# Half the blocks of attention weights transposed by VectorE and DMAs, in a two-layer RG-LRU and forgetting-attention trunk

## The chip, the cores and the metric

The kernel runs on one core of a Trainium2 chip. The metric is device time in microseconds (us) of one execution. A change is judged by the medians of runs of both kernels on the same chip. Engines are named as in the profile: PE (TensorE, matmuls), PEld (its weight loads), DVE (VectorE), ACT (ScalarE), POOL (GpSimd), SP (SyncE, which issues all the DMAs here).

## What is computed

The input x is 1024 positions by 1024 channels, in float32. Two residual layers and a last RMS norm are applied to it. Layer 0 is an RG-LRU branch of width 1536: a projection into a stream and a gate, a causal convolution of 4 taps, two block-diagonal gates, a linear recurrence along the sequence, a SiLU gate, and a projection back. Layer 1 is attention with 16 heads of 64, whose logits carry a bias of accumulated forget gates. Cut to what matters here:

```python
def fox_mixer(h, w_in, b_f, w_out):
    u = h @ w_in                       # q, k, v, gate (1024 each), 16 forget logits
    cum = cumsum(log_sigmoid(f_logit + b_f))
    # for each head and each block of 128 queries:
    logits = q_blk @ k.T / 8 + (cum_q - cum_k)
    p = softmax(where(kpos <= qpos, logits, -1e30))
    o = p @ v
    return (o * silu(gate)) @ w_out

def rms_norm(x, g):
    return x * rsqrt(mean(x * x) + 1e-6) * g
```

## The kernel before, in words

The whole kernel is transposed: channels lie on the 128 partitions, positions along the free dimension in two halves of 512. To keep the precision of float32, most operands are cut into a high part (a cast to the matmul's `fp32r`) and a low part (the rest, `to_hi` and `to_lo`, lines 84 to 98), and a product takes three matmuls: high by high, high by low and low by high. Raw weights land by DMA in tiles with the tag `wf` (4 buffers, lines 103, 268, 358, 532, 982) and are split into `wh` and `wl`.

**The norm.** `inv_rms` (line 142) sums squares with one-column matmuls (`col`), takes a root on ACT and a reciprocal on DVE, which gives one factor per position in a column `rms`. To have it as a row over all partitions, DVE multiplies the identity with each of the four columns (line 153) and one matmul with a matrix of ones turns that into `row` (lines 154 and 155). It is called four times.

**Layer 0** fills the first 455 us of the trace. Its loop over 12 blocks of channels loads raw weights, splits them and keeps PE supplied with projections.

**Layer 1.** `values` makes v for four heads at a time, `kq_units` makes q and k for a pair of heads, `g_units` the gate of a pair. For a head `hd` and a half `c` of the queries:

- `maxima(hd, c)` (line 708) takes four blocks of 128 queries, i = 4c to 4c+3, called rows here. For each, PE writes the scores S of the block against all (i+1) x 128 keys up to it, DVE masks them and finds the largest (line 731), and ACT writes the weights `p` = exp(...) into SBUF with their sums (line 736). Queries lie on the partitions.
- `weigh(hd, c)` (line 767) needs keys on the partitions. For two blocks of keys at a time, PE transposes each 128x128 block of `p` into PSUM (line 793, tile `pt`), ACT casts a high part `ph` (line 798), DVE subtracts a low part `pl` (line 801), and PE multiplies both with v into O (lines 781 and 782). The products of one step are issued only behind the transposes of the next step. Over a head there are 36 blocks to transpose.
- `scale` and `gated` multiply by the gate and the reciprocal sums on POOL. The result `yo` of a pair of heads is written to memory for the first six pairs (`y1d`, line 826). At heads 12 and later it is loaded again (`load_y`, line 861), split into parts (`split_loaded`, line 866), and multiplied with the output weights (`partial`, line 890).

The order on PE is written out by hand. In `run` and `ordered` (lines 838 to 850) a string is read letter by letter: "0" takes a step of `weigh`, "1" a row of `maxima`, "." two blocks (six matmuls) of projection work as fill. For heads 0 to 11 the two strings of a head are

```python
ORDER = "1.0.1.1.1.0.0", "10.1.0.1.01.0.0"
run(first, weigh(hd, 0), maxima(hd, 1), fill=fill)
run(second, weigh(hd, 1), maxima(hd + 1, 0), fill=fill, side=side)
```

and `LAST`, with more fill between, serves heads 12 to 15. The steps of PE are tied to this order by `tc.issue_after(pe[0].ins)`. The order on the other engines, SP's queue among them, is found by the framework's scheduler at build time. S and `pt` share two PSUM buffers (tag `S`, two banks each), O has two. Each row's `p` has one buffer of its own (`p0` to `p7`), `ph` and `pl` have three.

Of the kernel before, what the change touches and what calls it, by code (L numbers as in the profile page):

```python
# [17 lines left out]
P = 128  # L18
SEQ = 1024
# [19 lines left out]
def trunk(ctx: ExitStack, tc: tile.TileContext, xt, w0, wg, wo0, pc, gn, gf, w1, wv, wf, bf, wo1, out):  # L39
# [60 lines left out]
    def split_weights(src, shape, hi_eng, lo_eng, parts=wpool):  # L100
        n = shape[0] * shape[1]
        room = -(-n // 64) * 64
        a = wpool.tile([P, room], F32, tag="wf", name="wf", bufs=4)[:, :n]
        b = parts.tile([P, room], F32R, tag="wh", name="wh")[:, :n]
        c = parts.tile([P, room], F32R, tag="wl", name="wl")[:, :n]
        wt, hi, lo = (t.rearrange("p (a b) -> p a b", a=shape[0]) for t in (a, b, c))
        for part, sl in src:
            nc.sync.dma_start(wt[:, :, sl], part)
# [70 lines left out]
    with ExitStack() as l0:  # L179
# [87 lines left out]
        def split_gates(n):  # L267
            wt = wpool.tile([P, 4, P], F32, tag="wf", name="wgf", bufs=4)[:, :2]
# [87 lines left out]
        def out_weights(g, d0, parts=wpool):  # L356

            wt = wpool.tile([P, 4, P], F32, tag="wf", name="wf", bufs=4)
            for j in range(2):
# [137 lines left out]

    y1d = dram.tile([2, KT, P, HALF], F32, name="y1d")
    cumd = dram.tile([HEADS, 2, SEQ], F32, name="cumd")
    recd = dram.tile([HEADS, 8, P], F32, name="recd")  # L500

    with ExitStack() as l1:
# [24 lines left out]
        def value_weights(g, parts):  # L527

            waiting = []
            for k in range(0, KT + 2, 2):  # L530
                if k < KT:
                    wt = wpool.tile([P, 2, 256], F32, tag="wf", name="wf", bufs=4)
                    nc.sync.dma_start(wt, wv[g, :, k : k + 2])
                    waiting.append(wt)
# [105 lines left out]

        fz = const.tile([P, 8, HEADS], F32, name="fz")
        Vs = {}
# [7 lines left out]
        def forget(half):  # L650
# [7 lines left out]
            e_ = at.tile([HEADS, HALF], F32, tag="ph", name="e", bufs=3)  # L658
            parts = [at.tile([HEADS, HALF], F32R, tag=f"p{i + 2 * half}", name="cp", bufs=1) for i in (3, 4)]
            hi, lo = parts  # L660
# [45 lines left out]
        stats, ps_ = {}, {}  # L706

        def maxima(hd, c):

# [4 lines left out]
            sums = stats[hd]  # L714
            for i in range(4 * c, 4 * c + 4):
                n = (i + 1) * P
# [5 lines left out]
                for lo_, hi_ in ((0, min(n, HALF - o_)), (HALF - o_, n)):  # L722
# [11 lines left out]

                p = ps_[i] = at.tile([P, n], F32, tag=f"p{i}", name="p", bufs=1)
                seen[0] = nc.scalar.activation(  # L736
                    p, S[:, :n], AF.Exp, bias=m, scale=-1.0, accum_out=sums[:, i : i + 1]
                )
                yield
            if hd == HEADS - 1 or c == 1:  # L740
# [26 lines left out]
        def weigh(hd, c, sub=slice(0, HALF)):  # L767
# [9 lines left out]
            def products(j0, qlo, parts):  # L777
                for j, q, (ph, pl) in zip((j0, j0 + 1), qlo, parts):
# [3 lines left out]
                    matmul(o, v, pl, start=False, stop=j == nj - 1)  # L782

            held = None
            for j0 in range(0, nj, 2):
                A = ps.tile([P, 2, HALF], F32, tag="S", name="pt")
                qlo = [max(begin, j * P) for j in (j0, j0 + 1)]
                ns = [end - q for q in qlo]
                for jj in range(2):
                    ks = slice((j0 + jj) * P, (j0 + jj + 1) * P)  # L790
                    for q in range(qlo[jj], end, P):
                        o = q - qlo[jj]
                        transpose(A[:, jj, o : o + P], ps_[q // P][:, ks], ident)
                parts = []
                for jj in range(2):
                    a = A[:, jj, : ns[jj]]
                    ph, pl = (at.tile([P, HALF], F32R, tag=t, name=t, bufs=3)[:, : ns[jj]] for t in ("ph", "pl"))
                    to_hi(ph, a, nc.scalar)
                    parts.append((ph, pl))
                for jj, (ph, pl) in enumerate(parts):  # L800
                    to_lo(pl, A[:, jj, : ns[jj]], ph, nc.vector)
                if held:
# [11 lines left out]
        def gated(hd, c, sub=slice(0, HALF)):  # L814
# [10 lines left out]
            elif hd < 13:  # L825
                nc.sync.dma_start(y1d[c, pair], yo)

# [38 lines left out]
        def split_loaded(c):  # L866
            for pair in range(6):
                yh, yl = y1[c][pair]
                with tc.issue_after(seen[0].ins):
                    to_hi(yh, f32(yl), nc.scalar)  # L870
                with tc.issue_after(masked[0].ins):
                    to_lo(yl, f32(yl), yh, nc.vector)
                yield

        def beside(steps, first, more):

            for i, _ in enumerate(steps):
                if i >= first:
                    next(more, None)
                yield  # L880

# [39 lines left out]
        def turned(c, q):  # L921
# [9 lines left out]
            else:  # L931
                res = [tu.tile([P, SEQ], F32, tag="U1", name="res"), at.tile([P, SEQ], F32, tag="p7", name="res", bufs=1)]
            for b in range(2):
# [43 lines left out]
        def late():  # L977

            for half in range(2):
                wh, wl = (kqpool.tile([P, 8, P], F32R, tag=f"qk{p}{half}", name=f"wo{p}") for p in "hl")  # L980
                for b in range(2):
                    wt = wpool.tile([P, 4, P], F32, tag="wf", name="wf", bufs=4)
                    for d in range(2):
# [24 lines left out]
        for hd in range(HEADS):  # L1008
            pair = hd // 2
            if hd % 2 == 0:  # L1010
                if hd < 12:
                    fill = kq_units(pair + 1, ((1, (0, 1)), (0, (0,))))
                elif hd == 12:
                    pairs = ((0, 1), (2, 3), (4, 5), (6, 7))
                    todo = [(db, c) for two in pairs for c in range(2) for db in two]
                    splits = [split_loaded(c) for c in range(2)]
                    fill = chain(
# [122 lines left out]
```

## Time and profile before

| what | us |
|---|---|
| median of 3 runs | 1113.87 (1113.86 to 1114.06) |
| profiled execution, its own time | 1113.94 |
| its span, first to last instruction | 1112.2 |
| PE busy | 1101.9 |
| DVE busy | 755.0 |
| ACT busy | 582.4 |
| POOL busy | 166.1 |

In the rows of the profile, L57 is the line of the helper that issues every matmul and L61 that of the transposes, so work is told apart by tile: `gps` and `ups` are projections, `vps` v, S scores, `pt` the weights' transposes, O the products with v, `ops` output projections. "x7" after a name is a count of instructions, "a <- b" after a wait names what ended it. A busy time is a union of spans, so instructions that overlap count once.

### The profile page before, as it was taken

The page shows a single profiled execution, that of the slowest core. Times are in us where ns is not written, and L with a number is a line of the kernel's source. Part 1 is how long each engine was busy: PE and PEld are TensorE (multiplying, and loading weights), DVE is VectorE, ACT ScalarE, POOL GpSimd, SP SyncE. Part 2 cuts the span into 40 slices and gives each one's busy share as a digit, 9 for nine tenths or more (in the row PEclk, how much of TensorE's full clock was granted, in tenths as well). Part 3 has the DMA queues.
Part 4 walks back from the last instruction along what each step waited for, and adds up shares of the span by engine and source line. Part 5 has one row for each costly group of instructions (what it writes and reads, how often), then busy time and mean ns, then how long its engine had stood idle before and what let it go on. Part 6 is the DMA issues. An engine that isn't in the chain of part 4 may idle for free.

```text
span 1112.2 us, 15778 instructions
## 1 busy us (share of the span) xinstructions
PE 1101.9 (99%) x5697; PEld 935.1 (84%) x5697; DVE 755.0 (68%) x1266; ACT 582.4 (52%) x1075; POOL 166.1 (15%) x120
## 2 busy tenths in 40 slices
PE   9999999999999999999999999999999999999997
PEld 7787888888888888988888988889888898878886
DVE  8888755876669687756676566765667655576645
ACT  8487445355453665544555355544555544454435
POOL 1222212111111201421110100101002020010110
PEclk9999999999999999999999999999999999999999
DMA  6111111111112113443334224242142431655444
GB/s 239 48 57 43 51 54 43 48 53 42 62 35 75 48 54 129 129 112 118 101 90 103 91 69 109 72 113 96 53 122 75 103 108 38 185 159 185 142 147 189
DMA packets 63558, 105.43 MB, mean 95 GB/s; under 512 B 9364, under 2 KB 24340, under 8 KB 63480
## 3 DMA queue, kind: packets, MB, share of 16 engines
q1 hardware_dynamic: 63480, 104.42, 31.1%
q8 instruction: 45, 0.74, 0.3%
q14 instruction: 33, 0.27, 0.1%
HBM read 63.30 MB, written 15.93 MB: 71 GB/s over the span
## 4 chain that ended last, share of the span: by engine, by line
PE 93%; issue 3%; DVE 1%; ACT 1%; POOL 1%; DMA 1%; SPq 0%; DVEq 0%; POOLq 0%; ACTq 0%
PE gps L57 33%; PE ops L57 17%; PE ups L57 10%; PE vps L57 8%; PE S L57 6%; PE O L57 6%; PE pt L61 6%; PE turn L57 3%; PE gate L57 2%; POOL wl L98 1%; PE sscol L57 0%; DMA x<-in_xt 0%; DVE hl L232 0%; PE rsrow L57 0%; DMA wf<-in_w 0%
## 5 line engine op out<-in xcount | busy, mean ns | idle before, releaser
L57 PE MATMUL gps<-hh,wh 128*128 128x512 f32 x576 | 228.2, 396 | 0.0
L57 PE MATMUL gps<-hh,wl 128*128 128x512 f32 x576 | 225.6, 392 | 0.2 <-POOL wl L98 0.2
L57 PE MATMUL gps<-hl,wh 128*128 128x512 f32 x576 | 225.5, 392 | 0.0
L87 ACT CAST wh<-wf 128x512 fp32r<-128x512 f32 (+2 forms) x156 | 94.0, 607 | 141.8 <-PE gps L57 56.0
L736 ACT ACTIVATE p<-S,m 128x128 f32<-128x128 f32 (+7 forms) x128 | 94.9, 741 | 140.0 <-DVE m L731 139.1
L98 POOL TENSOR_TENSOR wl<-wf,wh 128x512 fp32r<-128x512 f32 (+1 forms) x60 | 95.6, 1600 | 382.2 <-ACT wh L87 321.7
L98 DVE TENSOR_TENSOR pl<-pt,ph 128x512 fp32r<-128x512 f32 (+1 forms) x198 | 98.7, 540 | 77.0 <-ACT ph L87 76.3
L57 PEld LDWEIGHTS gps<-hl,wh 128*128 128x128 f32 x576 | 108.2, 188 | 23.8
L57 PEld LDWEIGHTS gps<-hh,wl 128*128 128x128 f32 x576 | 108.5, 188 | 19.2 <-POOL wl L98 0.6
L57 PEld LDWEIGHTS gps<-hh,wh 128*128 128x128 f32 x576 | 108.5, 188 | 19.0
L731 DVE CUSTOM_DVE_ANT_0 S<-S,mask 128x128 f32<-128x128 f32 (+7 forms) x128 | 97.3, 760 | 34.2 <-PE S L57 29.6
L765 POOL TENSOR_TENSOR sg<-sg,recb 64x512 f32<-64x512 f32 x32 | 42.8, 1356 | 441.9 <-DMA recb<-recd 407.3
L87 ACT CAST ph<-pt 128x512 fp32r<-128x512 f32 (+1 forms) x198 | 83.5, 472 | 29.1 <-PE pt L61 23.9
L57 PE MATMUL S<-T,U 96*128 96x512 f32 (+7 forms) x384 | 91.7, 347 | 0.0
L98 DVE TENSOR_TENSOR wl<-wf,wh 128x512 fp32r<-128x512 f32 x96 | 68.3, 719 | 24.6 <-ACT wh L87 23.8
L375 DVE TENSOR_TENSOR x<-x,ops 128x512 f32<-128x512 f32 x80 | 54.1, 681 | 40.3 <-PE ops L57 40.3
L57 PEld LDWEIGHTS S<-T,U 128*128 128x128 f32 (+1 forms) x384 | 68.7, 189 | 12.5 <-ACT p L736 0.2
L61 PE MATMUL pt<-ident,p 128*128 128x128 f32 x576 | 79.2, 273 | 0.0
L61 PEld LDWEIGHTS pt<-ident,p 128*128 128x128 f32 x576 | 67.5, 140 | 11.5 <-issue 2.1
L57 PE MATMUL ups<-hh,wh 128*128 128x512 f32 x192 | 75.4, 394 | 1.0 <-ACT hh L89 0.4
L57 PE MATMUL ups<-hh,wl 128*128 128x512 f32 x192 | 75.0, 391 | 0.6 <-POOL wl L98 0.6
L57 PE MATMUL ups<-hl,wh 128*128 128x512 f32 x192 | 75.2, 391 | 0.2 <-DVE hl L232 0.2
(163 smaller groups left out, 2245.4 us busy)
## 6 DMA issues: line engine op xcount, KB each, us to landing
wf<-in_w SPq DMA_DIRECT2D x100, 256.0 KB
wf<-in_wo SPq DMA_DIRECT2D x64, 128.0 KB
U<-qkh SPq DMA_DIRECT2D x64, 128.0 KB
T<-qkh SPq DMA_DIRECT2D x28, 256.0 KB
x1d<-x SPq DMA_DIRECT2D x16, 256.0 KB
wf<-in_wv SPq DMA_DIRECT2D x16, 256.0 KB
U<-qkl SPq DMA_DIRECT2D x32, 128.0 KB
xp<-x1d SPq DMA_DIRECT2D x16, 256.0 KB
```

Of the source, the lines that this page charges most:

```text
L57: pe[0] = nc.tensor.matmul(*args, **kw)
L61: pe[0] = nc.tensor.transpose(*args)
L87: nc.scalar.copy(hi, src)
L98: return eng.tensor_tensor(lo, src, f32(hi), ALU.subtract)
L375: nc.vector.tensor_tensor(x, x, pt, ALU.add)
L731: masked[0] = nc.vector.tensor_tensor_reduce(S[:, :n], S[:, :n], mask[:, SEQ - n :], -1.0, -NEG, ALU.add, ALU.min, accum_out=m)
L736: seen[0] = nc.scalar.activation(p, S[:, :n], AF.Exp, bias=m, scale=-1.0, accum_out=sums[:, i : i + 1])
L765: nc.gpsimd.tensor_tensor(sg, sg, recs[hd // 2][rows, part], ALU.mult)
```

## The change

Rows 2, 3, 6 and 7 of a head, that is two of each four, no longer go through PE for most of their blocks. After exp, `turn_row` has DVE transpose the row's weights in blocks of 32x32 within each quarter of the partitions, into a tile `turn` (one buffer), and SP writes it to memory (`turnd`). When the second row of a pair is written, four DMAs, one for each group of 32 partitions of the result, read both rows back in such an order that the blocks stand transposed, over the place where the rows were (`two_rows`). This covers 3 blocks of keys of rows 2 and 3 and 7 of rows 6 and 7. The last block of rows 3 and 7 and all of rows 0, 1, 4 and 5 stay with PE. Rows 2 and 3 of head 0 stay with PE as well (`by_dma`). `maxima` takes its four rows from the last to the first.

In `weigh` each step now has a near part, from PE's transposes in PSUM, and a far part, from SBUF. Each is split by its own cast and subtraction, near parts first.

`inv_rms` drops the multiplications with the identity and the matmul with ones; four transposes of the column, read as a 128x128 tile by broadcast, write the row.

The results of the first six pairs of heads are split into high and low as soon as they are made, and both parts are written to memory and loaded later; `split_loaded` and `beside` go.

To make room, `wf` has 3 buffers in place of 4, and some small tiles share other tags.

```diff
-        a = wpool.tile([P, room], F32, tag="wf", name="wf", bufs=4)[:, :n]
+        a = wpool.tile([P, room], F32, tag="wf", name="wf", bufs=3)[:, :n]
...
-        nc.vector.reciprocal(rms, rms)
+        done = nc.vector.reciprocal(rms, rms)
+        row = ps.tile([P, HALF], F32, tag="O", name="rsrow")[:, : nb * P]
         for b in range(nb):
-            done = nc.vector.tensor_scalar(rs[:, b * P : (b + 1) * P], ident, rms[:, b : b + 1], None, ALU.mult)
-        row = ps.tile([P, HALF], F32, tag="O", name="rsrow")[:, : nb * P]
-        inst = matmul(row, onesf, rs, start=True, stop=True)
+            inst = transpose(row[:, b * P : (b + 1) * P], rms[:, b : b + 1].to_broadcast([P, P]), ident)
...
+        two_rows = {}
+        turnd = [dram.tile([P, 2, (4 * c + 3) * P], F32, name=f"turnd{c}") for c in range(2)]
+        def row_tile(i, n):
+            c, r = i // 4, i % 4 - 2
+            if r < 0:
+                return at.tile([P, n], F32, tag=f"p{i}", name="p", bufs=1)
+            size = (4 * c + 3) * P
+            if r:
+                two_rows[c] = at.tile([P, 2 * size + P], F32, tag=f"pp{c}", name="pp", bufs=1)
+            return two_rows[c][:, r * size : r * size + n]
+        def by_dma(hd, c):
+            return hd > 0 or c == 1
+        def turn_row(i, p):
+            c, r = i // 4, i % 4 - 2
+            nk = 4 * c + 3
+            t = at.tile([P, 7 * P], F32, tag="turn", name="turn", bufs=1)[:, : nk * P]
+            nc.vector.transpose(
+                t.rearrange("p (m k q) -> p k m q", m=4, q=32),
+                p[:, : nk * P].rearrange("p (k m q) -> p k m q", m=4, q=32),
+            )
+            nc.sync.dma_start(turnd[c][:, r], t)
+            if r == 0:
+                to = two_rows[c][:, : 2 * nk * P].rearrange("p (r b f) -> p r b f", r=2, b=4)
+                src = turnd[c].rearrange("(b p) r (m f) -> m p r b f", b=4, m=4)
+                for m in range(4):
+                    nc.sync.dma_start(to[32 * m : 32 * m + 32], src[m])
+        def far_rows(c):
+            return two_rows[c][:, : (8 * c + 6) * P].rearrange("p (b k q) -> p b k q", b=8, q=32)
...
-            for i in range(4 * c, 4 * c + 4):
+            for i in reversed(range(4 * c, 4 * c + 4)):
...
-                p = ps_[i] = at.tile([P, n], F32, tag=f"p{i}", name="p", bufs=1)
+                p = ps_[i] = row_tile(i, n)
...
+                if i % 4 > 1 and by_dma(hd, c):
+                    turn_row(i, p)
...
-                for jj in range(2):
-                    ks = slice((j0 + jj) * P, (j0 + jj + 1) * P)
-                    for q in range(qlo[jj], end, P):
-                        o = q - qlo[jj]
-                        transpose(A[:, jj, o : o + P], ps_[q // P][:, ks], ident)
...
+                near, far = [], []
+                for jj, j in enumerate((j0, j0 + 1)):
+                    rows = range(qlo[jj] // P, end // P)
+                    away = [i for i in rows if i % 4 > 1 and j < 4 * c + 3] if by_dma(hd, c) else []
+                    own = [i for i in rows if i not in away]
+                    for o, i in enumerate(own):
+                        transpose(A[:, jj, o * P : (o + 1) * P], ps_[i][:, j * P : (j + 1) * P], ident)
...
+                for lo in range(2):
+                    for (ph, pl), (src, to) in zip(parts, near):
+                        if to.stop:
+                            split(src, ph[:, to], pl[:, to], lo)
+                for lo in range(2):
+                    for (ph, pl), f in zip(parts, far):
+                        if f:
+                            j, b, to = f
+                            split(far_rows(c)[:, b, j], *(z[:, to].rearrange("p (b q) -> p b q", q=32) for z in (ph, pl)), lo)
...
-                nc.sync.dma_start(y1d[c, pair], yo)
+                yh = at.tile([P, HALF], F32R, tag="xp", name="yh", bufs=2)
+                with tc.issue_after(seen[0].ins):
+                    to_hi(yh, yo, nc.scalar)
+                with tc.issue_after(masked[0].ins):
+                    to_lo(yo.bitcast(F32R), yo, yh, nc.vector)
+                for part, y in enumerate((f32(yh), yo)):
+                    nc.sync.dma_start(y1d[c, pair, part], y)
...
-                nc.sync.dma_start(f32(pair_of_y(c, pair)[1]), y1d[c, pair])
+                for part, y in enumerate(pair_of_y(c, pair)):
+                    nc.sync.dma_start(f32(y), y1d[c, pair, part])
...
-                        beside(g_units(7, (1,)), 0, splits[0]),
+                        g_units(7, (1,)),
                         load_y(1),
-                        beside(beside(partial(todo), 0, splits[0]), 2, splits[1]),
+                        partial(todo),
```

More of the change, by code (lines that the diff above doesn't have):

```diff
@@ L658, in forget @@
             e_ = at.tile([HEADS, HALF], F32, tag="ph", name="e", bufs=3)
-            parts = [at.tile([HEADS, HALF], F32R, tag=f"p{i + 2 * half}", name="cp", bufs=1) for i in (3, 4)]
+            parts = [at.tile([HEADS, HALF], F32R, tag=t, name="cp", bufs=1) for t in (("p4", "p5"), ("pp1", "turn"))[half]]
             hi, lo = parts
@@ L782, in products, with split @@
                     matmul(o, v, pl, start=False, stop=j == nj - 1)
+            def split(src, hi, low, lo):
+                if lo:
+                    to_lo(low, src, hi, nc.vector)
+                else:
+                    to_hi(hi, src, nc.scalar)
             held = None
@@ L788, in weigh @@
                 ns = [end - q for q in qlo]
-                for jj in range(2):
-                    ks = slice((j0 + jj) * P, (j0 + jj + 1) * P)
-                    for q in range(qlo[jj], end, P):
-                        o = q - qlo[jj]
-                        transpose(A[:, jj, o : o + P], ps_[q // P][:, ks], ident)
[L794 to L801, printed above, removed]
+                near, far = [], []
[5 more added lines that the diff above has]
+                        transpose(A[:, jj, o * P : (o + 1) * P], ps_[i][:, j * P : (j + 1) * P], ident)
+                    w = len(own) * P
+                    near.append((A[:, jj, :w], slice(0, w)))
+                    far.append((j, slice(4 * (away[0] % 4) - 8, 8), slice(w, ns[jj])) if away else None)
+                parts = [
+                    tuple(at.tile([P, HALF], F32R, tag=t, name=t, bufs=3)[:, :n] for t in ("ph", "pl")) for n in ns
+                ]
+                for lo in range(2):
[7 more added lines that the diff above has]
+                            split(far_rows(c)[:, b, j], *(z[:, to].rearrange("p (b q) -> p b q", q=32) for z in (ph, pl)), lo)
                 if held:
```

28 lines of the change are left out of this document (7 added, 21 removed).

## Prediction

> **What bounds the kernel now.** I read the page's busy shares first, then the chain that ended last, then a table of windows cut at the heads of the attention stage.
>
> ```profile
> PE 1101.9 (99%) x5697; PEld 935.1 (84%) x5697; DVE 755.0 (68%) x1266; ACT 582.4 (52%) x1075; POOL 166.1 (15%) x120
> ```
> ```profile
> by line: PE gps L57 33.2%; PE ops L57 17.1%; PE ups L57 10.0%; PE vps L57 8.4%; PE S L57 6.4%; PE O L57 6.2%; PE pt L61 5.7%; issue 3.4%; PE turn L57 2.6%; PE gate L57 2.3%; POOL wl L98 0.7%; PE sscol L57 0.4%; DMA x<-in_xt 0.4%; DVE hl L23
> ```
> ```profile
> 531.90:561.30 29.40, 29.40 (x160) 25.09 (x159) 20.64 (x43) 16.32 (x37) 3.83 (x3) 1.00 0.48 126
> 561.30:590.90 29.60, 29.60 (x160) 24.98 (x159) 19.91 (x43) 15.69 (x36) 4.33 (x3) 1.00 0.27 73
> ...
> 964.75:1005.50 40.75, 39.55 (x202) 32.65 (x201) 31.40 (x60) 23.12 (x51) 4.61 (x3) 1.00 0.65 201
> ```
>
> Columns of the last fence: stretch, length, then busy time of PE, PEld, DVE, ACT and POOL, granted clock, DMA share, GB/s. The first two stretches are head 1 and head 2, each from its first score matmul in `maxima(hd, 1)` to the next head's. PE is busy in all of both and the granted clock is 1.00: no wait is on the path, the order of PE's own instructions is. So a matmul taken out is time gained, as long as nothing that PE needs comes later than it does now. The third stretch, head 13, has 1.2 us in which PE is idle. The other engines have room, but VectorE (DVE) not much: 40.55 of 59.0 us in the two heads.
>
> One head in the chain, piece by piece (start, length, what; head 2):
>
> ```profile
> 561.45 0.65 PE S L57 x4
> 562.10 1.42 PE gps L57 x6
> 563.51 0.76 PE pt L61 x7
> ...
> 565.66 0.71 PE S L57 x4
> ...
> 567.75 0.82 PE S L57 x4
> ...
> 569.95 0.93 PE S L57 x4
> ...
> 572.28 0.33 PE pt L61 x3
> ...
> 575.32 0.29 PE S L57 x2
> 575.61 0.88 PE pt L61 x8
> ...
> 577.89 0.24 PE S L57 x2
> ...
> 579.53 1.01 PE pt L61 x8
> 580.53 0.93 PE O L57 x4
> ...
> 582.83 0.34 PE S L57 x2
> ...
> 584.54 0.77 PE pt L61 x7
> ...
> 586.24 0.47 PE S L57 x2
> ...
> 588.12 0.33 PE pt L61 x3
> ```
>
> S are the score matmuls of one block of 128 queries ("row"), rows 4 to 7 and then the next head's 0 to 3; pt the transposes of the weights; O the products with v; gps the six matmuls of one "." of the hand-written order.
>
> **Transposes removed.** A head has 36: 0.76 + 0.33 + 0.88 + 1.01 + 0.77 + 0.33 = 4.08 us, 0.113 us each. Rows 2 and 3 lose 3 each, rows 6 and 7 lose 7 each: 20 of 36. Head 0 keeps those of its rows 2 and 3 (`by_dma`), so 16 x 20 - 6 = 314 go, and 314 x 0.113 = 35.5 us. By the chain's share, 5.7% of 1112.2 us over 576, one is 0.110 us and the gain 34.5. I take 35.5, since the runs left are as short as the x3 ones, which also give 0.11.
>
> The Trainium skill, "TensorE: Matmul & The Clock Gate", Part 4, gives about 390 ns for a lone 128x128 transpose and about 275 in a kernel. By 275 the gain would be 86 us and the sum 1031 us; these runs of back-to-back transposes show 0.113, and the measurement decides.
>
> **What is put in their place on DVE.** Two 32x32-block transposes of 896 columns and two of 384 a head, which the trace does not have. The nearest rows:
>
> ```profile
> 565.37 1.16 DVE L98 TENSOR_TENSOR pl<-pt,ph 128x512 fp32r<-128x512 f32 x2 [0.69 <-ACT ph L87]
> ...
> 568.61 1.10 DVE L731 CUSTOM_DVE_ANT_0 S<-S,mask 128x896 f32<-128x896 f32 x1 [1.15 <-PE S L57]
> ...
> 574.02 0.62 DVE L98 TENSOR_TENSOR pl<-pt,ph 128x256 fp32r<-128x256 f32 x2
> ```
> ```profile
> L342 DVE TENSOR_TENSOR_SCAN a<-a,ti 128x1024 f32<-128x1024 f32 x11 | 30.1, 2738 | 0.2
> ...
> L87 ACT CAST ph<-pt 128x256 fp32r<-128x256 f32 x43 | 15.3, 368 | 9.5 <-PE pt L61 4.8 <-issue 2.9 <-ACT sq L951 1.7
> ...
> L731 DVE CUSTOM_DVE_ANT_0 S<-S,mask 128x384 f32<-128x384 f32 x16 | 8.9, 557 | 1.6 <-PE S L57 1.6
> ...
> L1075 DVE TENSOR_SCALAR res<-res,ssq 128x1024 f32<-128x1024 f32 x4 | 2.7, 749 | 0.0
> ```
>
> The quickest wide form is 749 ns for 1024 columns (0.66 us for 896), the slowest the scan, 2738 (2.40 us for 896, 1.03 for 384). I take the mask pass, 1.10 and 0.56, since its 1.23 ns a column are near those of the plain subtractions (1.16 us for 1024). That is 3.3 us a head. The 8 extra low parts a head (near and far apart) cost little: two of 256 took 0.62, two of 512 took 1.16, so one cut adds about 0.04. The low parts of y, 0.58 each, add 1.2 a pair of heads. Two heads then ask DVE for 40.55 + 6.6 + 0.6 + 1.2 = 49 us, of 59.0 - 2 x 20 x 0.113 = 54.5: 90%, still under PE. ACT gains 8 casts a head and two for y; at 16.32 of 29.4 it has room.
>
> **The round trip.** Row 6's weights go exp, DVE, memory, back, split, and must be there for the first product of `weigh(hd, 1)`. The rows are now taken from the last to the first, so row 6 has the second place, at 565.66 above. From there to the first product at 580.53 is 14.87 us now. Shorter by ten transposes (two of three, four of eight, four of eight: 1.13), and by the places of rows 5 and 4 against rows 6 and 7 (0.82 + 0.93 - 0.71 - 0.65 = 0.39); longer by row 6's own (0.11) and the next head's rows 3 and 2 in place of 0 and 1 (0.47 + 0.34 - 0.29 - 0.24 = 0.28): 13.7 us are allowed. What it needs:
>
> ```profile
> 569.80 1.01 ACT L736 ACTIVATE p<-S,m 128x896 f32<-128x896 f32 x1 [1.31 <-DVE m L731]
> ```
> ```profile
> 575.38 0.26 SPq L750 DMA_DIRECT2D recd<-rc  x1
> ...
> 576.67 0.47 SPq L754 DMA_DIRECT2D recb<-recd  x1
> ```
> ```profile
> 581.30 2.54 POOL L765 TENSOR_TENSOR sg<-sg,recb 64x512 f32<-64x512 f32 x2 [15.47 <-DMA recb<-recd]
> ```
> ```profile
> 0.75 0.39 SPq L108 DMA_DIRECT2D wf<-in_w  x1
> ```
> ```profile
> 3.30 0.62 ACT L87 CAST wh<-wf 128x512 fp32r<-128x512 f32 x1 [1.07 <-DMA wf<-in_w]
> ```
> ```profile
> SPq L624 <- PE S L57: 50.7, 7, 13.1
> ...
> SPq L898 <- DMA x1d<-xp: 19.6, 12, 3.1
> ```
>
> Scores to the end of exp: 567.75 to 570.81, 3.06 us. Place in DVE's queue: 0 to 0.7, take 0.35. The transpose: 0.66 to 2.40, take 1.10. The write of 448 KB: the 4 KB `recd` had landed 1.3 us after its issue, as the read behind it then went out; a read behind a 256 KB write waited up to 3.1; take 2.6. The four reads of 224 KB: three issues of 0.5 us before the last, which then takes what a 256 KB read takes, 2.55 (`wf`, 0.75 to 3.30) to 4.63 (`recb`, 576.67 to 581.30): 4.1 to 6.1, take 5.0. First high part on ACT: 0.37. Sum 12.5 us, between 9.4 and 15.7. So it fits with 1.2 us to spare, or comes up to 2.0 late. A late split costs PE at the product, but also holds what stands behind it: the exp of the next head's row 2 on ACT, the mask pass of that row on DVE; PE needs their score buffer only about 2.3 us after the product. The transposes of rows 7 and 6 share one `turn` buffer: row 7's exp ends about 3.4 us after the head's start (0.3 more than row 6 needs, for its width), so its write lands near 3.4 + 1.1 + 2.6 = 7.1; row 6 starts 4.1 after the head (565.66 - 561.45, less three or four transposes, plus row 7's width) and its exp ends at 4.1 + 3.06 = 7.2: no wait by these values. Rows 3 and 2 have about 14 us before `weigh(hd+1, 0)` and are smaller. On SP's queue the reads wait for the second write, about 2.6 us, and T, U and weight loads wait behind; their tiles are loaded a head ahead. Heads 12 to 14 last about 40 us with more "." in between, so lateness counts for heads 0 to 11. I book 0.4 us each, 5 us.
>
> **The rest.** The norm row:
>
> ```profile
> 35.21 0.86 PE rsrow L57 x2
> ```
>
> Four calls of 0.86 us become 16 transposes of 0.113, 3.4 to 1.8: 1.6 gained; DVE's four multiplications a call go too. y kept in two parts takes 12 casts and 12 subtractions out of heads 12 to 14, where PE idled 1.2 us in head 13: gained, if the 24 loads in place of 12 come in time; else up to 5 lost (12 more of 256 KB at the 201 GB/s of that stretch are 15 us of transfer, of which I let a third show). One buffer less for raw weights: SP fetches one tile less ahead; a load takes 2.55 us, and a tile of four blocks serves 24 matmuls, 24 x 1.42 / 6 = 5.7 us; so 0 to 3 us in all, take 1.
>
> Sum against the profiled run (1113.94 us, span 1112.2 plus 1.7 around it; the median of the runs is 1113.87): 1113.9 - 35.5 - 1.6 - 1.2 + 5 + 1 = 1081.6, so 1082 us.
>
> **Rivals.** *DVE becomes the bound.* If the block transpose runs at the scan's pace, a head's four take 6.9 us and two heads ask for 40.55 + 13.7 + 1.8 = 56 us, more than PE's 54.5. With the waits that a full queue has, heads 0 to 11 stay near 59 a pair, and what is left is four heads' 20 x 0.113 and the small gains: about 12 us, 1102. For it: 90% is full even by my value. Against: no plain pass over a tile here runs at the scan's 2.67 ns per element.
>
> *The round trip sits behind a blocked SP queue: slower.* SP takes its DMAs in order, and T's reload waited 50.7 us in 7 times for scores, 7.2 at a mean, with nothing urgent behind it. If such a wait stands ahead of row 6's write or reads, the data are 7.2 - 1.2 = 6 us late in twelve heads: 72 us lost against 37 gained, 1149 us. It decides from 37 / 12 = 3.1 us late on, so from a round trip 4.3 us over my 12.5. Against: T's reload waits for the last score row, which is now the shortest and done 9.0 us after the head's start (569.95 - 561.45, less 0.45 of transposes, plus 0.28 of wider rows ahead, plus its own 0.65), within half a us of row 6's turn (7.2 + 0.35 + 1.10). The Trainium skill's "VectorE: DVE Perf Modes", Rules for kernel authors, says to use TensorE for a 128x128 transpose when the result may go to PSUM, as it does here; that speaks for this rival, and no row of the trace bears on it but the 0.113 above.
>
> *Gain and lateness cancel*: 3 us late a head, 1114.
>
> **How the numbers follow.** Forecast case 0.63, DVE bound 0.17, cancelling 0.04, slow 0.16. Without stalls and load costs the sum is 1075.6; at the dearest run's price for a transpose (1.01 / 8 = 0.126) it would be 4 us less; I set the lower end between, 1073. With the round trip at its long end, 2.0 us late in twelve heads, it is 1076.6 + 24 = 1101, the end of the forecast's own range. The DVE case reaches to 1111; the slow and the cancelling cases are left out: 1073 to 1111. Faster 0.80, within 0.2% (2.2 us, about what this kernel's measurement can tell from no change) 0.04, slower 0.16.
>
> **What would show it.** Right: 262 pt matmuls; heads 1 to 11 near 27.5 us with PE full; DVE near 90% there; block transposes of 896 near 1.1 us; PE's waits, where they are, in front of O behind far splits. Wrong: block transposes of 2 us and more, DVE without gaps; or long waits of ACT for DMA `pp<-turnd` and of PE for `ph`, with SP standing at T, U or wf loads while rows are turned; or new idle time of PE around 960 to 975 for `load_y`.

## The result and the profile after

The changed kernel takes 1179.43 us (median of 4 runs, 1177.51 to 1180.33) against 1113.88 for the one before on the same chip: 1.0586 times as long, with a 95% interval of 1.0567 to 1.0604. The forecast was 1082, with a range from 1073 to 1111. The profiled execution of the changed kernel is the run of 1177.51 us, with a span of 1175.4.

Busy shares first, then the chain that ended last, by line:

```profile
PE 1103.2 (94%) x5391; PEld 916.3 (78%) x5391; DVE 804.8 (68%) x1432; ACT 598.4 (51%) x1195; POOL 169.4 (14%) x120
```
```profile
PE gps L57 26%; PE ops L57 15%; PE ups L57 9%; PE vps L57 8%; PE S L57 5%; PE O L57 5%; DMA pp<-turnd 4%; DMA turnd<-turn 3%; PE turn L57 2%; PE gate L57 2%; SPq L737 2%; PE pt L61 1%; DVE pl L98 1%; POOL wl L98 1%; ACT pp L770 1%
```

The time outside PE's busy time (span less busy) is 1175.4 - 1103.2 = 72.2 us, against 1112.2 - 1101.9 = 10.3 before: 61.9 more. PE's busy time itself is 1.3 us up although 314 transposes have gone. Both halves need an explanation. Before, the chain had no transfer of this stage in it; now `pp<-turnd` and `turnd<-turn`, the two legs of the trip, are in it.

The table of windows, same columns as in the prediction, for heads 1, 2 and 13:

```profile
536.81:572.65 35.84, 30.32 (x139) 24.40 (x139) 23.48 (x57) 17.84 (x46) 3.81 (x3) 0.90 0.62 171
572.65:604.25 31.60, 29.57 (x139) 23.92 (x139) 24.60 (x56) 17.23 (x45) 4.00 (x3) 0.95 0.60 172
...
1012.71:1062.33 49.62, 39.15 (x181) 31.82 (x181) 28.02 (x60) 18.07 (x47) 4.27 (x3) 0.90 0.90 293
```

Head 1 went from 29.40 to 35.84 us, head 2 from 29.60 to 31.60, head 13 from 40.75 to 49.62. Two things differ in each row: PE is idle for 2 to 10 us, and the granted clock is under 1.00. DVE's part came out as forecast, 23.48 + 24.60 = 48.1 us for heads 1 and 2 where the prediction had 49, but in windows that are 67 us long instead of 54.5.

Who waited for whom (us in total, times, longest; one line each from PE, ACT, DVE and SP):

```profile
PE O L57 <- ACT ph L87: 45.3, 13, 10.1
...
ACT ph L87 <- DMA pp<-turnd: 60.1, 18, 9.3
...
DVE turn L728 <- DMA turnd<-turn: 8.4, 9, 2.1
...
SPq L737 <- DMA turnd<-turn: 31.6, 25, 2.4
```

ACT stands in front of a far cast until the returned rows have landed, and PE stands in front of the product that needs it. The chain in the second half of head 1 shows one such wait whole (start, length, what):

```profile
545.77 0.61 PE S L57 x4
546.38 0.33 SPq L620
...
547.45 5.58 DMA turnd<-turn
553.03 0.02 issue
553.05 0.60 SPq L737
...
555.57 4.63 DMA pp<-turnd
560.20 0.02 issue
560.22 0.41 ACT ph L87
...
560.68 2.11 PE O L57 x4
562.79 2.56 PE gps L57 x6
```

Row 6's write goes out at 547.4, right behind T's reloads on SP (L620 and L621 are two of them), and lands 5.58 us later; the four reads take 7.1 us from the first issue to the last landing. PE had its last instruction before the wait at 555.35, so it stood 5.3 us. After it, four products of O take 2.11 us where they took 0.93 before, and the six `gps` 2.56 instead of 1.42: the clock had fallen. The trace's clock records show stretches at a granted clock of 0.5, each 3.4, 6.8 or 10.2 us long, behind nearly all waits of 2 us and more: 69.3 us of them, against one of 3.0 at the end of the run before. Without the end they are 65 us, and PE was busy in 50 of these. At half the clock that is about 25 us more for the same work (an estimate), most of the reason why PE is as busy as before with some 37 us less to do. Some 13 us are left; the scores, which take longer outside these stretches too, make some 8 of them. The Trainium skill, "TensorE: Matmul & The Clock Gate", Part 1, says that the array falls to half its clock after an idle window of about 3.4 us and needs a busy one of that length to come back. The lengths of the stretches here agree, being one, two or three times 3.4 us. The waits need not be that long: of the eleven that were followed by such a stretch, six lasted between 1.98 us (at 591.10) and 3.31.

The new operations (line, engine, operation, shape; then busy time in all, mean ns of one, and idle time in front):

```profile
L728 DVE STREAM_TRANSPOSE turn<-pp 128x896 f32<-128x896 f32 x32 | 35.5, 1110 | 17.2 <-ACT pp L770 14.5 <-DMA turnd<-turn 2.5
L728 DVE STREAM_TRANSPOSE turn<-pp 128x384 f32<-128x384 f32 x30 | 17.1, 570 | 6.9 <-DMA turnd<-turn 5.9 <-ACT ph L87 0.7
L61 PE MATMUL pt<-ident,p 128*128 128x128 f32 x224 | 35.2, 273 | 0.6 <-DVE pl L98 0.6
L61 PE MATMUL pt<-ident,pp 128*128 128x128 f32 x38 | 9.7, 273 | 0.0
```

224 + 38 = 262 transposes are left on PE, and a block transpose takes 1.11 and 0.57 us: both as forecast. A transpose's mean of 273 ns overlaps with its neighbours; that is why the prediction went by the chain's 0.113.

### The profile page after: what moved, and what is told of

Its sections match the earlier page's. It is cut to its first block, busy times and chain, and to the rows that moved or that the text cites. A ratio compares the mean times of both kernels' runs of the same rounds, so it can differ in the third digit from the quotient of the medians.

```text
span 1175.4 us, 15846 instructions
## 1 busy us (share of the span) xinstructions
PE 1103.2 (94%) x5391; PEld 916.3 (78%) x5391; DVE 804.8 (68%) x1432; ACT 598.4 (51%) x1195; POOL 169.4 (14%) x120
## 4 chain that ended last, share of the span: by engine, by line
PE 76%; DMA 11%; DVE 4%; issue 3%; ACT 3%; SPq 3%; POOL 1%; ACTq 0%; DVEq 0%; POOLq 0%
PE gps L57 26%; PE ops L57 15%; PE ups L57 9%; PE vps L57 8%; PE S L57 5%; PE O L57 5%; DMA pp<-turnd 4%; DMA turnd<-turn 3%; PE turn L57 2%; PE gate L57 2%; SPq L737 2%; PE pt L61 1%; DVE pl L98 1%; POOL wl L98 1%; ACT pp L770 1%
## 5 line engine op out<-in xcount | busy, mean ns | idle before, releaser
L57 PE MATMUL gps<-hh,wh 128*128 128x512 f32 x576 | 232.5, 404 | 0.0
L98 POOL TENSOR_TENSOR wl<-wf,wh 128x512 fp32r<-128x512 f32 (+1 forms) x60 | 100.4, 1679 | 376.3 <-ACT wh L87 274.1
L57 PE MATMUL O<-ph,v 128*128 128x512 f32 (+1 forms) x198 | 73.8, 381 | 45.3 <-ACT ph L87 45.3
L765 DVE CUSTOM_DVE_ANT_0 S<-S,mask 128x512 f32<-128x512 f32 (+7 forms) x128 | 96.8, 756 | 26.1 <-PE S L57 25.9
L98 DVE TENSOR_TENSOR pl<-pp,ph 128x256 fp32r<-128x256 f32 x157 | 71.2, 471 | 55.4 <-ACT ph L87 49.8
L57 PE MATMUL S<-T,U 128*128 128x512 f32 (+7 forms) x384 | 96.1, 359 | 8.5 <-ACT p L770 4.1
L87 ACT CAST ph<-pp 128x256 fp32r<-128x256 f32 x157 | 60.8, 410 | 69.6 <-DMA pp<-turnd 60.1
L770 ACT ACTIVATE pp<-S,m 128x512 f32<-128x512 f32 (+1 forms) x64 | 54.5, 852 | 60.0 <-DVE m L765 59.8
L57 PEld LDWEIGHTS O<-ph,v 128*128 128x128 f32 x198 | 39.1, 197 | 54.4 <-ACT ph L87 48.4
L57 PE MATMUL vps<-wh,hh 128*128 128x256 f32 (+1 forms) x256 | 74.2, 290 | 3.0 <-DVE qkl L98 2.7
```

What stands on the lines that cost most here:

```text
L57: pe[0] = nc.tensor.matmul(*args, **kw)
L87: nc.scalar.copy(hi, src)
L98: return eng.tensor_tensor(lo, src, f32(hi), ALU.subtract)
L765: masked[0] = nc.vector.tensor_tensor_reduce(S[:, :n], S[:, :n], mask[:, SEQ - n :], -1.0, -NEG, ALU.add, ALU.min, accum_out=m)
L770: seen[0] = nc.scalar.activation(p, S[:, :n], AF.Exp, bias=m, scale=-1.0, accum_out=sums[:, i : i + 1])
```

## The experiments

In the table, "against before" is each median less that of the kernel before, measured beside it on the same chip (between 1113.88 and 1114.39). x1, x4 and x6 are one run each; x9 and m2 have two.

| run | what it is | us | against before |
|---|---|---|---|
| after | the whole change | 1179.4 | +65.5 |
| x1_nowait | no wait for returned data | 1176.9 | +62.6 |
| x2_rest | nothing turned, the rest stays | 1134.9 | +20.5 |
| x3_one_row | only rows 3 and 7 turned | 1136.3 | +22.0 |
| x4_old_y | the change with y as before | 1180.7 | +66.3 |
| x5_no_trip | the change, no DMAs of the trip | 1117.0 | +3.0 |
| r_rev | before, rows reversed | 1128.1 | +14.1 |
| r_y | before, y in two parts | 1126.7 | +12.6 |
| r_norm | before, norm columns | 1115.5 | +1.5 |
| x6_free | DMAs, but neither wait | 1147.5 | +33.5 |
| x7_plain | no trip, old rows, old y | 1113.0 | -1.1 |
| m0_order | after, old y, later transposes | 1172.4 | +58.3 |
| x8_no_turn | x7 without block transposes | 1099.3 | -15.1 |
| r_wf | before, three raw buffers | 1114.8 | +0.4 |
| x9_free_old_y | x6 with the old y | 1132.3 | +17.9 |
| m2_pool | the trip on GpSimd's queue | 1225.1 | +110.7 |

**The first four** start from theory A, that the wait for the returned rows is the whole loss. They take this wait away, turn nothing at all, turn half as many rows (each read back by itself), and undo the change of y.

```diff
# x1_nowait
-  split(far_rows(c)[:, b, j], ...)
+  split(ident[:, :32].unsqueeze(1).to_broadcast([P, b.stop - b.start, 32]), ...)
# x2_rest
-  return hd > 0 or c == 1
+  return False
# x3_one_row
-  if i % 4 > 1 and by_dma(hd, c):
+  if i % 4 == 3 and by_dma(hd, c):
   # ... and the tiles, the write, the reads and `away` for one row in place of two
# x4_old_y: y1d, gated, load_y, split_loaded, beside as before the change
```

> The changed kernel, but the far splits read a constant (the identity, same widths) in place of the rows that come back from memory, so the round trip is made in full and nobody waits for it; the attention weights of half the blocks are left out of the result. Theory A (the data come back late, PE waits for them at the products, and its clock falls behind the waits): PE's waits for ph go, the granted clock is 1.00, 1076 to 1086 us. Rival B (the added work and traffic on DVE, ACT, SP and the DMA engines is what costs, whoever waits): over 1130 us.

Measured: 1176.94. Theory A falls: with ACT's wait gone, the time stays. The reason is in DVE's waits (first fence), most of them in front of the narrow block transposes (second), and in the timelines of DVE and SP around one of them (third):

```profile
DVE turn L728 <- DMA turnd<-turn: 48.9, 16, 5.0
```
```profile
L728 DVE STREAM_TRANSPOSE turn<-pp 128x384 f32<-128x384 f32 x30 | 17.1, 569 | 48.4 <-DMA turnd<-turn 46.5 <-ACT ph L87 1.9
```
```profile
518.79 0.50 SPq L786 DMA_DIRECT2D recd<-rc  x1
...
524.14 0.49 SPq L790 DMA_DIRECT2D recb<-recd  x1
524.72 4.60 SPq L732 DMA_DIRECT2D turnd<-turn  x2
...
528.40 0.58 DVE L728 STREAM_TRANSPOSE turn<-pp 128x384 f32<-128x384 f32 x1 [4.99 <-DMA turnd<-turn]
```

SP issues `recd` behind four reads of the trip, so that 4 KB land after 5.3 us; SP waits for them before `recb`; row 3's write stands behind that; row 2's block transpose needs the one `turn` buffer that this write holds; and on DVE the next low parts and mask pass stand behind the block transpose. PE is idle for 3.73 us from 527.05 on. A second wait had been standing behind the first, and nearly all of it, 46.5 of 48.9 us, is that of the narrow rows 2 and 3.

> The changed kernel with by_dma always false: every block is transposed by PE, nothing is turned; y in two parts, the norm factors by one-column transposes, three raw-weight buffers and the reversed rows stay. Theory A: the rest is worth what it was priced at, 1110 to 1114 us. Rival C (the loss of heads 13 and 14 is made by the doubled loads of y alone): over 1125 us, with PE idle in those heads.

Measured: 1134.87 (1133.41 to 1136.91). Theory A is off by 20 us: what the prediction had booked at -2 costs +20.5. The time lies in rival C's range, but not for its reason: heads 12 to 14 lose 2.8 us together and heads 0 to 11 lose 16.0.

> Only rows 3 and 7 are turned, row by row (half the bytes a read), rows 2 and 6 stay with PE: 157 fewer transposes than before. Row 7 is the first row of its head, so its round trip has about 4 us longer than row 6's, and its reads are half as large. Theory A: no waits of PE for ph in heads 0 to 12, gain 157 x 0.113 = 17.7 us: 1094 to 1100 us, up to 1110 if the loads of y still stand in front of the reads in heads 13 and 14. Rival B: half of the loss stays, about 1145 us.

Measured: 1136.30 (1133.5 to 1139.59). This is nearer to rival B. Half as many rows halve what the trip moves, but PE's waits still come to 32.9 us. Little of that is for far casts (1.1); most is in front of scores (13.4), transposes (8.1) and output projections (6.0).

> The changed kernel with y of the six pairs written whole, loaded once and split late, as before the change. Theory A: heads 0 to 11 wait as in the changed kernel; in heads 13 and 14, where 24 loads of y stood on SP's queue ahead of a row's write and reads, periods fall from 49.6 and 47.8 to about 42: about 1163 us. If the loads of y did not matter: 1175 to 1180 us.

Measured: 1180.66. With y as before, the whole change is no faster, though y costs 12.6 by itself (r_y). By heads, two effects cancel: heads 12 to 14 take 131.6 us instead of 135.4, but heads 0 to 11 take 477.4 instead of 470.2. Why the latter grow was not traced.

**The parts alone, and no trip.** For what the turning costs, theory T names two full waits, ACT's for the returned rows and DVE's for the turn buffer, and theory E the added work on DVE and ACT itself. For x2's 20 us, theory R names the reversed rows and theory Y the casts of y.

```diff
# x5_no_trip
-  nc.sync.dma_start(turnd[c][:, r], t)
-  if r == 0:
-      ...
-      for m in range(4):
-          nc.sync.dma_start(to[32 * m : 32 * m + 32], src[m])
# r_rev (on the kernel before)
-  for i in range(4 * c, 4 * c + 4):
+  for i in reversed(range(4 * c, 4 * c + 4)):
# r_y, r_norm, r_wf: the lines of the change on y, on root_mean, on bufs=4, on the kernel before
```

> The changed kernel without its write and its reads: rows 2, 3, 6 and 7 are still turned by blocks on VectorE and still split apart from the rest, but nothing goes to memory and the far splits read the row as exp left it, unturned (that part of the computation is left out). Theory T (the trip: two full waits in engines that work strictly in order, ScalarE's for the returned rows, 60.1 us, and VectorE's for the one turn buffer, which only showed at 48.9 us when the first was taken away): no such wait is left, so the time is that of the run in which nothing was turned, 1134.9, less 314 transposes of 0.113, 35.5, plus a little for the extra splits, about 1100, between 1095 and 1108. Theory E (the added work itself fills VectorE and ScalarE, where near splits and mask passes stand behind far splits and block transposes): above 1125.

Measured: 1117.04 (1114.59 to 1119.0). The trip as a whole is 62.4 us, nearly all of the loss. But what is left is not 1100 either: of the 35.5 us to be gained, 17.6 do not show, so both theories hold a part.

> The kernel before with its score rows taken from the last to the first, and nothing else. Theory R (the reversed order makes up most of the 20 us that the change costs with nothing turned, since the next row's scores wait for the exp of a wider row): 1127 to 1133. Theory Y (the casts of y in two parts make it up, standing on ScalarE behind GpSimd's product): 1113 to 1118.

Measured: 1128.09, ratio 1.0112 to 1.0140. Heads 0 to 11 lose 8.4 us together and head 14 loses 5.1. With the widest row first, its exp stands behind two casts on ACT, and the next row's scores wait for that exp. In head 2, at row 2 of the next head:

```profile
580.36 0.63 PE L57 MATMUL S<-T,U 128*128 128x384 f32 x2 [0.50 <-ACT p L736]
```

There are six such waits, 3.0 us together; the rest of the 8.4 was not traced. In head 14 PE waits 2.3 us for a late low part of the output weights, with a stretch at half the clock behind it.

> The kernel before with y of the six head groups cut into two parts when it is made, written and read as two, and nothing else. Theory R: 1112 to 1119. Theory Y: 1127 to 1133, with VectorE idle behind the cast of yh in odd heads.

Measured: 1126.66, ratio 1.0102 to 1.0130. Both theories hold a part again: 14.1 and 12.6, which with 1.5 (r_norm) and 0.4 (r_wf) make 28.6 where x2 has 20.5, so the parts overlap. In r_y the window of head 1 and its timeline show the mechanism, engine by engine:

```profile
531.60:565.10 33.50, 31.13 (x160) 26.22 (x158) 20.65 (x44) 16.98 (x38) 3.82 (x3) 0.95 0.45 119
```
```profile
555.24 1.28 POOL L820 TENSOR_TENSOR yo<-yo,sg 128x512 f32<-128x512 f32 x1
...
556.56 0.62 ACT L87 CAST yh<-yo 128x512 fp32r<-128x512 f32 x1 [1.82 <-POOL yo L820]
...
557.21 0.69 DVE L98 TENSOR_TENSOR yo<-yo,yh 128x512 fp32r<-128x512 f32 x1 [3.18 <-ACT yh L87]
...
559.03 0.69 DVE L731 CUSTOM_DVE_ANT_0 S<-S,mask 128x512 f32<-128x512 f32 x1
...
560.64 0.55 PE L61 MATMUL pt<-ident,p 128*128 128x128 f32 x3 [2.37 <-ACT p L736]
```

The product with the gates waits for the reciprocal sums (`recd` and `recb`, the "norm factors" of the expectations). The cast on ACT waits for the product, the low part on DVE for the cast, and the mask pass of a score row that was done at 556.9 stands behind the low part on DVE. Head 1 goes from 29.4 to 33.5 us, of which 2.4 are PE's idle time and the rest its clock (0.95 in that window).

> The kernel before with the norm factors turned by one-column transposes, and nothing else. The prediction's 1.6 us gained: 1112.3, between 1111.8 and 1113.9.

Measured: 1115.49 (11 runs), ratio 1.0007 to 1.0025: no gain. The four multiplications a call that DVE no longer has to do let its queue come in another order at the start of the stage, and one new wait gives back more than the 1.6 us:

```profile
PE vps L57 <- DVE qkl L98: 2.7, 1, 2.7
```

**What in the trip costs, and what is left without it.** x6 takes both waits away and keeps the DMAs; x7 drops the trip, the row order and y together; m0 gives row 6 more time.

```diff
# x6_free: x1's line, and
-  nc.sync.dma_start(turnd[c][:, r], t)
+  nc.sync.dma_start(turnd[c][:, r], p[:, : nk * P])
# x7_plain: x5's and x4's lines, and rows in the old order
# m0_order: x4's lines, and
-  ORDER = "1.0.1.1.1.0.0", "10.1.0.1.01.0.0"
+  ORDER = "1.1.0.1.1.0.0", "1.1.0.10.10.0.0"
```

> The changed kernel with both waits of the trip taken away and all its DMAs kept: the far splits read a constant tile instead of the returned rows, and the write goes out from the row as exp left it, so that the one turn buffer is never held (half of the attention weights are left out of the result by that). Theory T (the two waits are what the trip costs): within 15 us of the run without the trip, 1117, so 1110 to 1132. Theory Q (the six DMAs a turned pair of rows put in SP's one queue, and their traffic, make the loads of scores, weights and norm factors late): 1150 or more, as with the first wait alone taken away, 1177.

Measured: 1147.54, between the two. Taken away in this order, the waits are 32 us of the trip's 62, and the DMAs without them 30.

> The changed kernel without the trip, with its score rows in the old order and y written whole and cut late: what is left of the change is 314 TensorE transposes fewer, block transposes and far splits in their place (which read the row as it is, so that part of the computation is left out), the norm columns and one raw weight buffer fewer. If the three dear parts are the trip, the row order and y, this is the prediction's own sum without its stalls, 1113.9 less 35.5 and about 2 more for norm and weights: 1077 to 1086. If the added instructions on VectorE and ScalarE cost time where they stand, which the 17.6 us missing in the run without the trip would be: 1094 to 1103.

Measured: 1112.99 (1111.71 to 1116.03), ratio 0.9983 to 1.0002. It lies above both ranges, and it is the most telling run: with no trip at all, and the rows and y as before, nothing is gained. The window of head 2, then DVE and PE in the first half of head 3, where the same wait comes in each head:

```profile
563.50:591.80 28.30, 27.50 (x139) 22.87 (x139) 23.83 (x55) 16.16 (x44) 4.27 (x3) 1.00 0.31 88
```
```profile
602.16 1.11 DVE L728 STREAM_TRANSPOSE turn<-pp 128x896 f32<-128x896 f32 x1
603.19 0.65 DVE L611 SCALAR_TENSOR_TENSOR qkl<-gps,qkh 128x512 fp32r<-128x512 f32 x1
603.77 1.09 DVE L728 STREAM_TRANSPOSE turn<-pp 128x896 f32<-128x896 f32 x1
604.78 0.13 DVE L774 TENSOR_SCALAR sums<-sums 128x8 f32<-128x8 f32 x1
604.82 0.28 DVE L98 TENSOR_TENSOR pl<-pt,ph 128x128 fp32r<-128x128 f32 x1
605.02 0.75 DVE L98 TENSOR_TENSOR pl<-pp,ph 128x256 fp32r<-128x256 f32 x2
...
605.49 0.39 PE L57 MATMUL O<-pl,v 128*128 128x256 f32 x1 [0.80 <-DVE pl L98]
```

PE's busy time in head 2 is 27.50 us, just where the prediction had the head; but DVE, at 84%, reaches the low parts only after two block transposes, and PE waits 0.80 us for them, up to 1.4 in some heads, 11.9 us in 14 waits. The 12 heads up to 11 gain 5 us together instead of 26, and heads 12 to 14 lose 4.9 (124.1 against 119.2).

> The changed kernel with y whole and cut late, and in the hand-written order the first transposes of weigh one score row and a dot or two later in both halves of a head, so that row 6 has about 3.9 us more before its split stands in ScalarE's queue (row 6's scores come earlier too, 2.1 us after row 7's). If lateness of the returned rows, 14.3 to 19.0 us against some 13.7, is what counts, it is now covered in most heads: 1105 to 1135. If the wait for the one turn buffer, or SP's queue, takes its place: 1140 to 1175.

Measured: 1172.41 (1169.92 to 1176.33), 8 us better than x4. The wait moves: it now stands in front of the transposes of the next block, again held by DVE's low parts, which wait for the returned rows.

```profile
PE pt L61 <- DVE pl L98: 35.6, 9, 5.4
```

With 3.9 us more, row 6 still comes late, since its trip took 16.6 to 20.1 us in heads 1 to 11 of this run.

**The last four.**

```diff
# x8_no_turn: x7's lines, and turn_row left empty
# x9_free_old_y: x6's and x4's lines
# m2_pool (on the changed kernel)
-  nc.sync.dma_start(turnd[c][:, r], t)
+  nc.gpsimd.dma_start(turnd[c][:, r], t)
   ...
-  nc.sync.dma_start(to[32 * m : 32 * m + 32], src[m])
+  nc.gpsimd.dma_start(to[32 * m : 32 * m + 32], src[m])
```

> The run without the trip, in the old row order and with the old y, 1113.0, now without the block transposes on VectorE too; the far splits stay and read the row as it is (so half of the weights are left unturned). Theory D (the block transposes, 35.5 us of VectorE in all, stand in front of mask passes and low parts): 1080 to 1092, which is the prediction's sum without its stalls. Theory S (the far splits themselves, 8 more casts and 8 more subtractions a head, which the products wait for): 1104 to 1114.

Measured: 1099.28 (1097.92 to 1099.7), ratio 0.9849 to 0.9881. This lies between the two (the expectation counted the 896-wide block transposes alone; with the others they are 52.6 us of DVE). The block transposes cost 14 us where they stand, and x7's waits of O for low parts are gone with them. Head 2 is at 28.09 us:

```profile
561.71:589.80 28.09, 27.78 (x140) 22.73 (x139) 21.78 (x51) 16.11 (x44) 4.45 (x3) 1.00 0.32 88
```

Some 20 us of the 35.5 are still missing: 10.1 in heads 0 to 11 (16.3 gained where 234 x 0.113 = 26.4 were to come, 14 transposes going in head 0 and 20 in each of the others), 7.6 in heads 12 to 14 (120.0 us, 119.2 before, less 6.8 to come), and 2.7 in r_norm's wait. Which of the far casts, the far subtractions and the thinner buffers does it in heads 12 to 14 was not separated.

> The kernel before with three buffers for raw weights in place of four, and nothing else. The prediction's 0 to 3 us: 1113.5 to 1117. If fewer buffers cost loads in heads 12 to 14, where weights and y are fetched together: up to 1122.

Measured: 1114.80 (10 runs), ratio 0.9994 to 1.0013: no difference that can be told.

> The changed kernel with both waits of the trip taken away and its DMAs kept (far splits read a constant tile, the write goes out from the row), and y whole and cut late. Theory C (in odd heads the norm factors come late through SP's queue, GpSimd's product waits for them, ScalarE's cast of y for that, and mask passes and exps stand behind it): 1117 to 1128. Theory L (loads of scores and weights late behind the trip's DMAs): still 1140 to 1150.

Measured: 1132.28 (1130.83 to 1133.72), between the two and 15.3 below x6. Theory C's path is there: in head 1 of x6 the data of `recd` are ready at 551.6, but SP issues it at 554.0, behind loads that stood behind the four reads; the cast of y comes at 564.14, and PE waits 3.38 us for a cast `ph` behind it. With y as before, heads 1, 5 and 9 are 15.6 us shorter. But x5, which has no DMAs of the trip, is already 8.2 longer there than x9, so by this estimate only some 7 of the 30 us come from y and the DMAs meeting. The rest stays with y as before, in PE's waits for late casts and low parts.

> The changed kernel with the write and the four reads of the trip issued from GpSimd's queue instead of SP's. If SP's queue in order is a large part of the trip's cost: 1140 to 1163. If the trip's own length (exp, place on VectorE, write, reads) is what counts: 1165 to 1190, since the reads still take what they take and GpSimd's products of the gates now stand behind them.

Measured: 1225.08, above both ranges. GpSimd's queue holds its own products of the gates, and the trip's DMAs stand behind them and they behind the trip's waits:

```profile
583.57 1.29 POOL L871 TENSOR_TENSOR yo<-yo,sg 128x512 f32<-128x512 f32 x1 [3.72 <-DVE yo L862]
587.92 0.62 POOL L732 DMA_DIRECT2D turnd<-turn  x1 [3.06 <-DVE turn L728]
...
596.76 0.61 POOL L737 DMA_DIRECT2D pp<-turnd  x1 [2.81 <-ACT ph L87]
...
606.54 2.75 POOL L801 TENSOR_TENSOR sg<-sg,recb 64x512 f32<-64x512 f32 x2 [6.60 <-DMA recb<-recd]
609.24 0.60 POOL L732 DMA_DIRECT2D turnd<-turn  x1
```

The profile counts these DMAs under another kind of queue (`software_dynamic`), so the run changes more than the place in line.

Of the versions with a real trip the nearest to the kernel before is x3, 22.0 us slower, and the best without one leaves the turning out. A second `turn` buffer was not tried.

## Why the prediction was wrong, point by point

**Right in size.** 262 transposes left; 0.113 us each (PE's busy time of head 2 in x7, 27.50, is where the sum had the head); a block transpose of 1.11 and 0.57 us; 48 us of DVE in two heads; one buffer less, +0.4.

**The step that failed first: the round trip, and what lateness costs.** The prediction had 12.5 us needed, 13.7 allowed, and booked 0.4 us a head, 5 us in all. The trip costs 62.4 us (x5), and heads 0 to 11 take 470.2 us together where they took 423.0. In heads 1 to 11 of the changed kernel row 6 takes 14.3 to 19.0 us from its scores to the last landing (28.2 in head 13). By the terms of the sum, with what was taken in brackets: scores to the end of exp 3.8 to 4.0 (3.06, from the old order, where row 6 came behind the narrower row 5); place on DVE 0.1 to 1.5 (0.35); block transpose 1.11 (1.10); write 2.4 to 2.7 in even heads, 3.6 to 5.6 in odd ones (2.6); reads 6.4 to 7.3 (5.0). The write is late in odd heads because T's and U's reloads go out just around it; the reads because the four mostly land about 1 us apart, while SP issues them 0.61 us apart, so the transfers and not the issues set the pace. The range given, up to 15.7, stopped short of the odd heads.

The price of being late was the larger error. A head that is 2 to 5 us late loses that, then up to half of a stretch of 3.4 or 6.8 us to the clock. And the waiting instruction holds its whole engine: with ACT's wait taken away, DVE's for the turn buffer brings the same total (x1). The prediction worked that wait out for rows 7 and 6 alone ("no wait by these values"), where it nearly held; for rows 3 and 2, which make 46.5 of x1's 48.9 us, it looked at the time until their use and not at the buffer. The slow rival had the place right, SP's queue among the causes, and its turning point too (4.3 us over 12.5, which most odd heads pass); its own reason, T's wait for scores ahead of the write, is not what was seen. What held SP was its own trip: reads waiting for the write, and `recb` for a `recd` that stood behind reads.

**"Still under PE."** 90% of DVE was taken as room. Even with no trip, no reversed rows and the old y, what is left of the change eats nearly all of the 35.5 us (x7: 1112.99). 14 of it are the block transposes (x8): PE waits for low parts that stand behind block transposes of 1.1 us, 11.9 us in x7 and none in x8. 2.7 are the norm columns' wait, and some 18 stay open. The Trainium skill, "VectorE: DVE Perf Modes", Rules for kernel authors, sends a 128x128 transpose with a PSUM destination to TensorE. This case agrees, with nothing gained in x7: not by the price of one, but by what stands behind it on VectorE.

**The two parts of y**, booked as 1.2 gained, cost 12.6 alone. The casts were moved out of heads 12 to 14 to a place where ACT has to wait for GpSimd's product, with mask passes and exps behind; the prediction counted them only as work ("ACT gains 8 casts a head and two for y").

**The reversed rows** were counted inside the round trip only. By themselves they cost 14.1. A likely reason, seen in part in r_rev's waits, is that the hand-written order was laid out for rows that grow.

**The norm columns**: 1.6 was right for PE (it is 1.7 us less busy with `rsrow`), but 2.7 come back as one wait.

## What to carry to other kernels

An engine that is 84% busy, as DVE in x7, is not free: for each instruction that is added to its queue, name what stands behind it and who waits for that. Price a transfer out and back at its longest case, with the other loads of that moment on the same queue. Being late costs more than the lateness: here TensorE's clock fell, and the next wait stood behind the first. Price each part alone before adding them up: the small parts here make 28.6 us one by one and 20.5 together.

## What the runs showed of the hardware

In the changed kernel TensorE's granted clock was 0.5 in steps of 3.4 us behind its waits. Waits of 1.98 and 2.81 us were followed by one step and one of 2.04 by none, most waits between 3 and 5.3 us by two (one of 4.95 by one), and one of 10.1 by three. A 4 KB write took 5.3 us to land behind 896 KB of reads on the same queue (x1). Issuing the trip from GpSimd's queue instead of SP's made the kernel 46 us slower (m2).
